# Half-array products of four mixing branches issued in pairs, and products with the meta keys issued last

## The chip, the cores and the metric

The kernel runs on one core of one Trainium2 chip. The metric is the device time of one execution in microseconds (us), the median of several runs. TensorE is written PE, its weight loads PEld; VectorE is DVE, ScalarE is ACT, GpSimd is POOL, SyncE is SP.

## The reference

The model has two blocks; the change touches only the first. Its input is 16 meta tokens followed by 256 tokens, T = 272 rows of 1024, and it runs two layers. In each layer a normed input goes through one wide projection into four mixing branches, whose outputs are gated, summed and projected; a feed-forward part follows. Cut to the branches:

```python
# A: differential attention, 4 heads, two maps m of width 64, values of width 128
s = einsum('bqhmd,bkhmd->bmhqk', q, k) * 64 ** -0.5
p = softmax(s + bias);  a = p[:, 0] - lam * p[:, 1];  o = a @ v
# B: gated linear attention, 4 heads, keys of width 64, values of width 128, chunks of 64, two directions
att = (q_dec @ k_in.T) * causal;  o = att @ v + q_dec @ S_start
# C: latent attention, 4 heads, 128 plain + 64 rotary columns
s = q_nope @ k_nope.T + q_pe @ k_pe.T;  o = softmax(s * 192 ** -0.5) @ v
# D: windowed attention, 8 query heads on 2 key heads of width 64, one sink per head
o = softmax([s_band, s_meta, s_sink]) @ v
```

All four see the 16 meta keys beside the 256 others. The second block (adaptive norms, gated feed-forward parts, a convolution mixer, a pooling mixer with another attention) is unchanged.

## The kernel before, in words

Everything that is multiplied on a large scale (projections, feed-forward parts) is a product split into three parts of the type fp32r (`mm3`: high by high, high by low, low by high); in the profile these are the matmuls whose output is a PSUM buffer `g`. The weights stream in through SP, ACT makes the high part of each (`wh`), DVE the low part (`wl`).

The branches are Python generators (`gen_a` to `gen_d` in `mixing`). A generator emits one step of a branch and yields a number; `tick` resumes it after that many ticks, and between two ticks the main program emits half a tile of a projection, 12 matmuls into `g`. So each engine gets one fixed order in which steps of a branch lie between runs of 12, 24 or 36 matmuls into `g`. Only where the main program needs a branch (`finish`) do its last steps follow each other without such runs between them.

The branches' own products are plain fp32 matmuls into PSUM buffers `a` (`aps`, four buffers; each holds 512 columns of 128 partitions). In the trace each of them is two matmul records, called two passes here. A product whose stationary operand has 64 rows, or whose output has 64 columns, uses half of the PE array; its place follows from the partitions on which operand and output lie.

- Scores (`scores`, and `units`, which runs score, exponential and transpose of successive units one after another): for the query blocks A and B (128 queries each) a unit makes four score tiles 128x272 and DVE adds the bias and takes the maximum (line 566). For block M (the 16 meta queries) one tile holds all four heads, 32 partitions each.
- In `gen_a` a unit is one map m of all four heads: the rows `64*m` to `64*m+63` of `qa` and `ka`. After the second map `close` joins the two, and `transposed` turns the result for the products with the values (`pT` for the 256 tokens, `pm` for the meta keys, `vt` and `vm` the values).
- In `gen_d` and `gen_c` and in the output products of `gen_a` the third product of each head is the one with the meta keys (`pm`, `vm`, 16 rows).
- In `gen_b` heads alternate between rows 0 to 63 and 64 to 127 (`r`), one head after another; `kr` in `gen_c` likewise.

## Time and profile before

| | |
|---|---|
| median of 3 runs | 2278.74 us (2277.09 to 2283.06) |
| profiled execution, its own time | 2284.18 us |
| its span, first to last instruction | 2281.6 us |
| mean granted clock of TensorE | 0.978 of full speed |
| busy: PE, DVE, ACT, POOL | 2192.9, 1612.5, 1217.2, 240.6 us |

Busy times are sums over the span. Matmuls are pipelined: one lasts longer than the step to the next, so time is read from starts of successive rows, not from durations. A row of the timeline merges successive instructions of one form; its first number is the start, its second the time from there to the end of the last.

### The profile page before, as it was taken

The numbers are of one execution on the slowest core, as the hardware profiler recorded it, in microseconds if no ns is written. First come the engines' busy times: TensorE is split into PE (matmuls) and PEld (weight loads), VectorE is DVE, ScalarE is ACT, GpSimd is POOL, SyncE is SP. The second block draws the span as 40 slices with busy tenths as digits, with TensorE's granted clock in tenths as the row PEclk, the third lists the DMA queues.
The fourth block names the chain that finished last, engine by engine and source line by source line (L and its number), as shares of the span: only waits on it lengthen the run. The fifth ranks groups of instructions, "written<-read, shape, count | busy, mean of one in ns | idle before, by whom it ended". The sixth has DMA issues, their size and how long they took to land. (4 is left out here: it accounts for less than half of the span.)

```text
span 2281.6 us, 41972 instructions
## 1 busy us (share of the span) xinstructions
PE 2192.9 (96%) x17048; PEld 2070.0 (91%) x17048; DVE 1612.5 (71%) x2809; ACT 1217.2 (53%) x2221; POOL 240.6 (11%) x285
## 2 busy tenths in 40 slices
PE   7999999999999999999999899986999999999998
PEld 7888888899988798788999799986999999989998
DVE  5655454798885555547989887798877787778553
ACT  4555244577556544445775554465644554466442
POOL 0220111100031001112000100066100000001000
PEclk9999999999999999999999899997999999999999
DMA  7553233454764343324657687733687687744551
GB/s 271 190 183 114 100 102 114 172 206 170 278 242 158 112 148 107 112 97 172 227 184 289 260 302 273 255 111 111 229 283 277 241 303 272 268 174 140 206 177 70
DMA packets 73618, 439.21 MB, mean 192 GB/s; under 512 B 14285, under 2 KB 15629, under 8 KB 25936
## 3 DMA queue, kind: packets, MB, share of 16 engines
q1 hardware_dynamic: 62736, 419.66, 51.3%
q0 software_dynamic: 10400, 16.79, 2.5%
q8 instruction: 133, 2.18, 0.4%
q14 instruction: 61, 0.50, 0.1%
q10 hardware_dynamic: 288, 0.07, 0.0%
HBM read 433.12 MB, written 10.01 MB: 194 GB/s over the span
## 5 line engine op out<-in xcount | busy, mean ns | idle before, releaser
L227 PE MATMUL g<-uh,wh 128*128 128x256 f32 (+2 forms) x3560 | 1034.0, 290 | 18.9 <-ACT uh L322 6.2
L227 PE MATMUL g<-ul,wh 128*128 128x256 f32 (+2 forms) x3560 | 1025.1, 288 | 9.5 <-DVE ul L326 5.9
L227 PE MATMUL g<-uh,wl 128*128 128x256 f32 (+2 forms) x3560 | 1021.8, 287 | 2.7 <-DVE wl L122 2.7
L122 DVE TENSOR_TENSOR wl<-raw,wh 128x1024 fp32r<-128x1024 f32 (+2 forms) x660 | 785.8, 1196 | 274.2 <-ACT wh L114 273.7
L114 ACT ACTIVATE wh<-raw 128x1024 fp32r<-128x1024 f32 (+2 forms) x660 | 670.2, 1020 | 335.5 <-PE g L227 298.9
L227 PEld LDWEIGHTS g<-uh,wh 128*128 128x128 f32 x3560 | 680.1, 191 | 42.2 <-issue 13.5
L227 PEld LDWEIGHTS g<-ul,wh 128*128 128x128 f32 x3560 | 678.7, 191 | 14.0 <-DVE ul L326 6.9
L227 PEld LDWEIGHTS g<-uh,wl 128*128 128x128 f32 x3560 | 680.7, 191 | 3.7 <-DVE wl L122 3.4
L227 PE MATMUL g<-gh,wh 128*128 128x256 f32 (+1 forms) x1056 | 299.2, 283 | 0.0
L227 PE MATMUL g<-gh,wl 128*128 128x256 f32 (+1 forms) x1056 | 299.2, 283 | 0.0
L227 PE MATMUL g<-gl,wh 128*128 128x256 f32 (+1 forms) x1056 | 299.1, 283 | 0.0
L227 PEld LDWEIGHTS g<-gl,wh 128*128 128x128 f32 x1056 | 201.5, 191 | 0.0
L227 PEld LDWEIGHTS g<-gh,wh 128*128 128x128 f32 x1056 | 201.3, 191 | 0.0
L227 PEld LDWEIGHTS g<-gh,wl 128*128 128x128 f32 x1056 | 201.3, 191 | 0.0
L1717 DVE CUSTOM_DVE_ANT_0 adaw<-adaw,condb,vec 128x1024 f32<-128x1024 f32 x144 | 182.4, 1280 | 1.5 <-DMA adaw<-in_ada_t_dram 1.5
L1620 DVE SCALAR_TENSOR_TENSOR y<-edge,vec,y 128x272 f32<-128x272 f32 (+1 forms) x176 | 86.4, 493 | 28.5 <-ACT y L1615 25.4
L227 PE MATMUL g<-oh,wh 128*128 128x272 f32 (+1 forms) x296 | 87.9, 297 | 0.0
L227 PE MATMUL g<-ol,wh 128*128 128x272 f32 (+1 forms) x296 | 84.6, 286 | 0.0
L227 PE MATMUL g<-oh,wl 128*128 128x272 f32 (+1 forms) x296 | 84.5, 285 | 0.0
L1863 ACT ACTIVATE sg<-g 128x256 f32<-128x256 f32 x80 | 30.6, 382 | 99.9 <-PE g L227 99.8
L1224 ACT ACTIVATE gt<-g 128x272 f32<-128x272 f32 (+1 forms) x64 | 25.1, 392 | 107.7 <-PE g L227 107.7
L1252 POOL TENSOR_TENSOR merged<-merged,w 128x272 f32<-128x272 f32 (+1 forms) x48 | 37.9, 798 | 338.5 <-DVE w L1251 338.3
(377 smaller groups left out, 2434.2 us busy)
## 6 DMA issues: line engine op xcount, KB each, us to landing
raw<-in_weights_dram SPq DMA_DIRECT2D x294, 1024.0 KB, 4.9
adaw<-in_ada_t_dram SPq DMA_DIRECT2D x72, 1024.0 KB, 6.6
raw<-in_weights_dram SPq DMA_DIRECT2D x28, 768.0 KB, 4.8
skew<-scr POOLq DMA_DIRECT2D x6, 1086.0 KB, 22.7
h<-skew POOLq DMA_DIRECT2D x8, 544.0 KB, 4.4
h<-skew POOLq DMA_DIRECT2D x8, 512.0 KB, 5.4
condb<-cond SPq DMA_DIRECT2D x5, 512.0 KB, 4.7
hd<-h SPq DMA_DIRECT2D x2, 1088.0 KB, 9.1
```

Of the source, the lines that this page charges most:

```text
L114: self.nc.scalar.activation(h3[:, :, d0 : d0 + n], c.tile[:, :, c0 : c0 + n], AF.Copy)
L122: self.nc.vector.tensor_tensor(out=l3[:, :, d0 : d0 + n], in0=c.tile[:, :, c0 : c0 + n], in1=h3[:, :, d0 : d0 + n].bitcast(F32), op=SUB,)
L227: self.nc.tensor.matmul(out, lhsT, rhs, start=start, stop=stop, skip_group_check=True)
L1224: nc.scalar.activation(t[:, :rn], ps[:, :rn], AF.Tanh, scale=0.5)
L1252: nc.gpsimd.tensor_tensor(out=mg, in0=mg, in1=t, op=ADD)
L1620: nc.vector.scalar_tensor_tensor(out=y, in0=e[:, o : o + on], scalar=cw(i), in1=y, op0=MUL, op1=ADD)
L1717: self.nc.vector.tensor_tensor_reduce(out=t[:, i, :], in0=t[:, i, :], in1=self.condb, scale=1.0, scalar=self.v("ada_b_2", c), op0=MUL, op1 ...
L1863: nc.scalar.activation(t, ps[:, :SEQ], AF.Silu)
```

## The change

In branch A a unit of block A or B becomes two heads with both maps; their four score products go in the order map 0 (rows 0 to 63), map 1 (rows 64 to 127), each into its own buffer (`score.step = 2` tells `scores` to take two buffers at a time). `close` joins the maps in every unit, and `transposed` handles two heads at a time (`pair`), so it runs twice as often on half the data. The bias of such a unit comes in two DMA issues instead of one. In branch D the two heads that share an output buffer alternate. In B two heads alternate on the two row halves, and their output products go by kind. In C the four or two products of a kind go one after another. In A, B, C and D the products with the meta keys come after the others.

```diff
     def scores(...):
-        for i in range(nt):
-            ps = self.aps()
-            score(ps, i)
+        for i0 in range(0, nt, step):
+            pss = [self.aps() for _ in range(step)]
+            score(pss if step > 1 else pss[0], i0)
+            for i, ps in enumerate(pss, i0):
...
     gen_a:
-                    def f(ps, i):
-                        self.mm(ps[:, :T], qa[r, i, q0 : q0 + nq], ka[r, i, :])
+                    def f(pss, i):
+                        h = 2 * m + i // 2
+                        for j, ps in enumerate(pss):
+                            r = slice(64 * j, 64 * j + 64)
+                            self.mm(ps[:, :T], qa[r, h, q0 : q0 + nq], ka[r, h, :])
...
-                for h in range(4):
-                    self.mm(o, pT[:, 0, h, q0 : q0 + nq], vt[:, 0, c], True, False)
-                    self.mm(o, pT[:, 1, h, q0 : q0 + nq], vt[:, 1, c], False, False)
-                    self.mm(o, pm[:, h, q0 : q0 + nq], vm[:, c], False, True)
+                for h, c in enumerate(cs):
+                    self.mm(ps[:nq, c], pT[:, 0, h, q0 : q0 + nq], vt[:, 0, c], h == 0, False)
+                    self.mm(ps[:nq, c], pT[:, 1, h, q0 : q0 + nq], vt[:, 1, c], False, False)
+                for h, c in enumerate(cs):
+                    self.mm(ps[:nq, c], pm[:, h, q0 : q0 + nq], vm[:, c], False, True)
...
     gen_d:
+                    for j in range(3):
+                        for i in range(2):
+                            o = ps[64 * i : 64 * i + 64, :T]
+                            if j < 2:
+                                self.mm(o, vt[:, j, c], pT[:, j, h, :], j == 0, False)
+                            else:
+                                self.mm(o, vm[:, c], pm[:, h, :], False, True)
...
     gen_b:
+                        for r, ps in zip(rows, pss):
+                            self.mm(ps[:, o : o + 128], ki[r, dp, t], qd[r, dp, t])
+                for d_ in range(2):
+                    for r, ps in zip(rows, psm):
+                        self.mm(ps[0:16, o : o + 16], ki[r, dp, 0:16], qd[r, dp, 0:16])
...
     gen_c:
+            def many(os, h0, q0, nq):
+                for h, o in enumerate(os, h0):
+                    self.mm(o, qn[:, h, q0 : q0 + nq], kn[:, h, :], True, False)
+                for h, o in enumerate(os, h0):
+                    self.mm(o, kr[r, 1 + h // 2, q0 : q0 + nq], kr[r, 0, :], False, True)
```

On PE, at the scores of branch C for block A in layer 0, before (a number behind `a_` is a buffer of its own; `kn` has 128 rows, `kr` 64):

```order
L227 MATMUL a_3620<-kn_3360,qn_3359 128x272
L227 MATMUL a_3620<-kr_3323 128x272
L227 MATMUL a_3624<-kn_3360,qn_3359 128x272
L227 MATMUL a_3624<-kr_3323 128x272
L227 MATMUL a_3628<-kn_3360,qn_3359 128x272
L227 MATMUL a_3628<-kr_3323 128x272
L227 MATMUL a_3632<-kn_3360,qn_3359 128x272
L227 MATMUL a_3632<-kr_3323 128x272
```

The same place on PE in the changed kernel:

```order
L227 MATMUL a_3630<-kn_3370,qn_3369 128x272
L227 MATMUL a_3631<-kn_3370,qn_3369 128x272
L227 MATMUL a_3630<-kr_3333 128x272
L227 MATMUL a_3631<-kr_3333 128x272
L227 MATMUL a_3638<-kn_3370,qn_3369 128x272
L227 MATMUL a_3639<-kn_3370,qn_3369 128x272
L227 MATMUL a_3638<-kr_3333 128x272
L227 MATMUL a_3639<-kr_3333 128x272
```

The eight products stand in four groups of a kind instead of eight, and the two `kr` products of a pair, on different row halves, now stand next to each other.

On PE, at the four meta products of branch B's output in layer 0, in the changed kernel (`vm,am` has 16 rows, `st,qdec` 64; before, the two kinds alternated head by head):

```order
L227 MATMUL a_3002<-vm_2556,am_2891 16x128
L227 MATMUL a_3003<-vm_2556,am_2891 16x128
L227 MATMUL a_3002<-vm_2556,am_2891 16x128
L227 MATMUL a_3003<-vm_2556,am_2891 16x128
L227 MATMUL a_3002<-st_2798,qdec_2464 16x128
L227 MATMUL a_3003<-st_2798,qdec_2464 16x128
L227 MATMUL a_3002<-st_2798,qdec_2464 16x128
L227 MATMUL a_3003<-st_2798,qdec_2464 16x128
```

One change of kind is left inside the step, and the `st` products alternate between the two row halves and two buffers.

## Rows read from the trace of the kernel before

**Rows 1.** The page: busy time of each engine, share of the span, instructions.

```profile
PE 2192.9 (96%) x17048; PEld 2070.0 (91%) x17048; DVE 1612.5 (71%) x2809; ACT 1217.2 (53%) x2221; POOL 240.6 (11%) x285
```

**Rows 2.** Stretches: PE, PEld, DVE, ACT, POOL busy, granted clock, DMA share, GB/s.

```profile
76.00:98.00 22.00, 21.84 (x149) 18.90 (x149) 19.19 (x64) 16.41 (x49) 2.41 (x3) 1.00 0.65 233
770.00:792.00 22.00, 21.44 (x144) 18.47 (x143) 16.75 (x53) 15.65 (x47) 0.75 (x1) 1.00 0.38 124
274.00:292.00 18.00, 18.00 (x103) 13.65 (x104) 4.32 (x9) 3.27 (x8) 2.05 (x2) 0.62 0.07 27
900.00:929.00 29.00, 28.41 (x223) 22.35 (x223) 12.46 (x26) 6.23 (x13) 3.49 (x4) 1.00 0.19 64
```

**Rows 3.** Timeline of PE, one unit of scores of branch A, layer 0.

```profile
70.52 2.10 PE L227 MATMUL a<-ka,qa 64*128 64x272 f32 x8
72.55 0.40 PE L227 MATMUL g<-uh,wh 128*128 128x272 f32 x1
```

**Rows 4.** Timeline of PE, scores in the pooling mixer of the second block.

```profile
2020.68 1.14 PE L227 MATMUL a<-k,q 64*128 64x256 f32 x8
2021.75 0.39 PE L227 MATMUL g<-uh,wh 128*128 128x256 f32 x1
```

**Rows 5.** Timeline of PE, scores of the meta queries of branch A.

```profile
62.89 0.66 PE L227 MATMUL a<-ka,qa 64*32 64x272 f32 x8
```

**Rows 6.** Timeline of PE, output products of branch A, blocks M and A.

```profile
101.62 0.61 PE L227 MATMUL a<-v,pT 128*16 128x128 f32 x4
...
102.48 0.61 PE L227 MATMUL a<-v,pT 128*16 128x128 f32 x4
...
106.77 0.71 PE L227 MATMUL a<-v,pT 128*128 128x128 f32 x4
107.41 0.48 PE L227 MATMUL a<-vm,pm 16*128 16x128 f32 x2
107.83 0.71 PE L227 MATMUL a<-v,pT 128*128 128x128 f32 x4
```

**Rows 7.** Timeline of PE, output products of branch D, one pair of heads.

```profile
153.81 1.13 PE L227 MATMUL a<-pT,v 128*64 128x272 f32 x4
154.87 0.67 PE L227 MATMUL a<-pm,vm 16*64 16x272 f32 x2
155.47 1.13 PE L227 MATMUL a<-pT,v 128*64 128x272 f32 x4
```

**Rows 8.** Timeline of PE, attention products of branch B, one head.

```profile
258.61 1.63 PE L227 MATMUL a<-qdec,kin 64*128 64x128 f32 x12
260.17 0.39 PE L227 MATMUL g<-uh,wh 128*128 128x272 f32 x1
```

**Rows 9.** Timeline of PE, output products of branch B, layer 1, blocks M and A.

```profile
914.71 0.37 PE L227 MATMUL a<-vm,am 16*16 16x128 f32 x2 [0.58 <-DVE am L1166]
...
915.33 0.39 PE L227 MATMUL a<-vm,am 16*16 16x128 f32 x2
...
919.76 0.49 PE L227 MATMUL a<-v,acs 128*128 128x128 f32 x2
920.18 0.66 PE L227 MATMUL a<-st,qdec 64*64 64x128 f32 x8
920.77 0.49 PE L227 MATMUL a<-v,acs 128*128 128x128 f32 x2
```

**Rows 10.** Timeline of PE, scores of branch C, blocks M and A.

```profile
330.08 0.65 PE L227 MATMUL a<-kn,qn 128*32 128x272 f32 x2
...
331.23 0.65 PE L227 MATMUL a<-kn,qn 128*32 128x272 f32 x2
...
337.86 0.73 PE L227 MATMUL a<-kn,qn 128*128 128x272 f32 x2
338.51 0.72 PE L227 MATMUL a<-kr 64*128 64x272 f32 x2
339.16 0.73 PE L227 MATMUL a<-kn,qn 128*128 128x272 f32 x2
```

## Prediction

> **What bounds the kernel now.** The first thing to read is the share of busy time: PE is busy for 96% of the span, the next engine, DVE, for 71% [rows 1]. That average hides the mixing layers, so the stretches come next. In 22 us around the scores of branch A in layer 0 PE is busy for 21.8 us, DVE for 19.2 and ACT for 16.4; in layer 1 for 21.4, 16.8 and 15.7 [rows 2]. PE ends last there too, but DVE is close behind it in layer 0. In the output products of branch B in layer 1 DVE has 12.5 of 29 us to do [rows 2].

> A busy PE is not a full PE, so the last view is the timeline of PE, step by step. Three things are to be seen in it.

> First, what a pass costs. The product of branch D with four passes lasts 1.13 us, the one with two 0.67 [rows 7], so a further pass of 272 columns is 0.23 us. With 128 columns the same difference is 0.71 against 0.48 [rows 6], or 0.11 us a pass.

> Second, half-array products that use the same rows or columns do not overlap, and those on different ones do. Eight passes of branch A's scores, all on one row half, take from 70.52 to 72.55, 2.03 us; eight passes of the pooling mixer's scores, whose heads alternate between the row halves and go to separate buffers, take from 2020.68 to 2021.75, 1.07 us [rows 3, 4]. They have 256 columns instead of 272, which over four rounds is some 0.05 us. For columns the meta queries of branch A show it: eight passes of 32 columns each, four places side by side, last 0.66 us in all [rows 5].

> Third, a change of kind (from 128 rows to 16 or 64, or back) stops the stream. One head of branch A's output takes 1.06 us from 106.77 to 107.83 [rows 6]; its six passes at 0.11 are 0.66. The rest, 0.40 us, is the way to the meta kind and back. I use it as the price of one round trip.

> **The change part by part.** The runs of matmuls into `g` between the steps keep their number, so what a step loses on PE is lost from the span, as long as nothing else becomes late. Each saving is for one step, times its number in two layers.

> Scores of A, blocks A and B: eight passes become four rounds of two. Before 2.03 us, after 1.07 + 0.05 = 1.12 [rows 3, 4]: 0.91 us, 8 units, 7.3 us.

> Output of A: for block M a head takes 0.86 us from 101.62 to 102.48; four are 3.43. Grouped: one head's 0.86 and 18 more passes at 0.11, 2.82; saved 0.6, twice, 1.2. For A and B four heads are 4 × 1.06 = 4.24; grouped 1.06 + 18 × 0.11 = 3.04; saved 1.2, 4 times, 4.8 [rows 6]. Together 6.0 us.

> Output of D: one head takes 1.06 us for its `pT` passes and 0.60 for the meta ones [rows 7], and its partner, on the other 64 columns, as much again. Alternating, both run side by side, so one head's 1.66 us goes, less some 0.01 of stagger: 1.65, 8 times, 13.2 us. This is the largest term.

> Attention of B: a head takes 1.56 us, with two trips from the 128-column kind to the 16-column kind [rows 8]. Two heads side by side take the passes of one and one trip less. A trip is bounded by nothing and 0.40; I take 0.2, since the small kind has only 16 columns to load. 1.56 + 0.2 = 1.76 per pair of heads, 4 pairs, 7.0 us. That the runs into `g` are entered half as often there I leave at nothing.

> Output of B: for M a head takes 0.62 us from 914.71 to 915.33, four 2.5; grouped 0.62 + 6 × 0.11 for the 16-row kind + 2 × 0.11 for the paired 64-row kind = 1.5; saved 1.0, twice. For A and B a head takes 1.01 us from 919.76, 0.42 of it up to the 64-row kind at 920.18 and 0.59 in it [rows 9]. There the column halves already overlap; after, four quarters do, so eight rounds serve four heads: 0.42 + 6 × 0.11 + 0.59 + 4 × 0.11 = 2.1 against 4.0; saved 1.9, 4 times. Together 9.6 us.

> Scores of C: for M a head takes 1.15 us from 330.08 to 331.23; four heads on four column places at once need little more than one: saved 3.4, twice. For A and B a head takes 0.65 us in each kind [rows 10]; a pair takes 0.65 + 2 × 0.23 for the full products, then 0.65 for both half ones: 1.76 instead of 2.60, saved 0.84, 8 pairs, 6.7. Together 13.5 us.

> Output of C: two heads share one round trip, 0.40, 4 pairs: 1.6 us.

> The sum is 7.3 + 6.0 + 13.2 + 7.0 + 9.6 + 13.5 + 1.6 = 58.2 us.

> What is added: per unit of A one more DMA issue on POOL, which is busy 11% of the span; per block two more, smaller evictions on ACT and one tiny multiply on DVE. They are hidden where DVE and ACT have room. In layer 0 DVE hardly has: three units of scores lie in 76 to 98 us, and 22 us less 3 × 0.91 is 19.3, against DVE's 19.2 [rows 2]. The transposes of A also come after every unit, so PE meets DVE's scaling four times a layer instead of twice. Nothing lost is the one end; all 7.3 us of A's scores and some in B (the wait for `am`, 0.58 us now [rows 9], has the work of two heads ahead of it in DVE's queue) the other, some 12 us. I take 3 us, near the lower end, because layer 1 has 16.8 us of DVE work for 19.3 us and the output steps right after give the queue time to empty.

> That leaves 55 us. The profiled execution's own 2284.2 less 55 is 2229; it lies 5.4 us above the median of the runs shown, so the forecast for the median is 2224 us.

> [...] In the changed scores of C the four `kr` products of block M use both row halves and write one buffer; in every other pair the row halves write separate buffers, as the rows of the pooling mixer do [rows 4]. No row here shows two row halves writing one buffer at a time. [...] If these rounds went one after the other instead, two more rounds of 0.23 us in each layer, 0.9 us, would be missing from the sum.

> **The rivals.** *Waits take more.* If A's units become bound by DVE and ACT in both layers and B waits longer for `am`, 12 us go: 46 us saved, 2233. For it speaks 19.2 of 22 us in layer 0; against it the 16.8 and 15.7 of layer 1 [rows 2].

> *The slow stretch goes away.* From 274 to 292 us, in B's output of layer 0, the granted clock averages 0.62; the same steps in layer 1, 900 to 929, ran at 1.00 [rows 2]. 18 × 0.38 is 6.8 us lost. Denser steps may keep the clock up there: 2217. Or the fall may move to another place, which changes nothing.

> *The pairs do not overlap.* Then only the grouping pays: A's and C's output keep 6.0 + 1.6; A's scores nothing; D gives back six passes a step, 2.2 left; B's attention gives back eight passes and the small ones, 2.8 left; B's output 5.2; C's scores 4.3. That is 22 us, 2257. Rows 3 and 4 differ in just this and speak against it.

> *Slower.* If the packed steps made the clock fall, work would take twice as long while it is down. 55 us more need some 110 us at half clock, eight times the 13.7 us that the mean of 0.62 over 18 us stands for [rows 2]; above that the kernel is slower than before, say 2290. For it speaks that the fall at 274 us came among half-array products. Against it: the same products ran at 1.00 in layer 1, and the change makes the share of full-array matmuls in these stretches larger. [...]

> **How the numbers follow.** The forecast 0.59 (its own range 2217 to 2231: waits from nothing to 10 us), more waits 0.15, the slow stretch gone 0.13, no overlap 0.05, slower 0.03; the last 0.05 is a partial overlap, between 2240 and 2257. The range from 2209 to 2239 holds the first three with 2 to 8 us of scatter and leaves out about 0.13. About 0.3%, 7 us, is what a measurement of this kernel can tell from no change: faster by more 0.96, within it 0.01, slower 0.03.

> **What would show it.** In the timeline after: A's scores x8 in some 1.12 us to the next `g`; D's output as one x8 of `pT` and one x4 of `pm` in 1.7 us; C's meta scores in 1.2 instead of 4.6; B's attention steps half as many. Wrong would be: x8 of `ka,qa` still 2 us (no overlap); rows of the transposes at the changed line with waits of over 0.5 us in most units of A (waits); a granted clock under 0.9 in stretches where it was 1.00.

## The result: 2219.6 us, 2.6% faster

The changed kernel takes 2219.61 us (median of 4 runs, 2218.51 to 2221.20), the kernel before 2278.6 beside it (4 runs, 2277.09 to 2283.06): a ratio of 0.9742, 95% interval 0.9726 to 0.9758. The forecast was 2224 within 2209 to 2239, so the kernel gained 59 us where 55 were forecast. The profiled execution took 2218.51 us, its span is 2216.7 us at a mean granted clock of 0.982.

The page of the changed kernel, its line of busy times; PE still has 96% [rows 1], of a shorter span:

```profile
PE 2127.1 (96%) x17048; PEld 2039.7 (92%) x17048; DVE 1611.7 (73%) x2813; ACT 1215.1 (55%) x2225; POOL 245.9 (11%) x293
```

The timeline of PE in the changed kernel (start, time to the end of the last, engine, line, operation and tiles, rows*columns, shape, count, idle time before and its releaser). In order: two units of A's scores and transposes behind them, A's output for blocks M and A, D's output, B's attention, C's scores for blocks M and A, C's output for two heads, and B's output in layer 1 for blocks M and A. The `g` row behind a step shows when it is over:

```profile
73.17 1.19 PE L227 MATMUL a<-ka,qa 64*128 64x272 f32 x8
74.29 0.39 PE L227 MATMUL g<-uh,wh 128*128 128x272 f32 x1
...
78.44 1.18 PE L227 MATMUL a<-ka,qa 64*128 64x272 f32 x6
80.09 0.72 PE L227 MATMUL a<-ka,qa 64*128 64x272 f32 x2 [0.46 <-ACT pm L653]
80.74 0.39 PE L227 MATMUL g<-uh,wh 128*128 128x272 f32 x1
...
83.18 0.66 PE L662 MATMUL a<-ident,s 128*128 128x128 f32 x4 [0.66 <-DVE mx L568]
...
99.08 1.92 PE L227 MATMUL a<-v,pT 128*16 128x128 f32 x16
...
101.90 0.40 PE L227 MATMUL g<-uh,wh 128*128 128x272 f32 x1
...
103.52 1.95 PE L227 MATMUL a<-v,pT 128*128 128x128 f32 x16
...
106.48 0.39 PE L227 MATMUL g<-uh,wh 128*128 128x272 f32 x1
...
149.21 1.14 PE L227 MATMUL a<-pT,v 128*64 128x272 f32 x8
150.28 0.67 PE L227 MATMUL a<-pm,vm 16*64 16x272 f32 x4
150.88 0.39 PE L227 MATMUL g<-uh,wh 128*128 128x272 f32 x1
...
247.39 1.36 PE L227 MATMUL a<-qdec,kin 64*128 64x128 f32 x24
248.68 0.40 PE L227 MATMUL g<-uh,wh 128*128 128x272 f32 x1
...
302.42 0.67 PE L227 MATMUL a<-kn,qn 128*32 128x272 f32 x8
303.02 0.66 PE L227 MATMUL a<-kr 64*32 64x272 f32 x8
303.61 0.39 PE L227 MATMUL g<-oh,wh 128*128 128x272 f32 x1
...
306.74 1.08 PE L227 MATMUL a<-kn,qn 128*128 128x272 f32 x4
307.75 0.73 PE L227 MATMUL a<-kr 64*128 64x272 f32 x4
308.41 1.18 PE L227 MATMUL a<-kn,qn 128*128 128x272 f32 x4
...
310.18 0.40 PE L227 MATMUL g<-uh,wh 128*128 128x272 f32 x1
...
328.89 2.00 PE L227 MATMUL a<-pT,v 128*128 128x272 f32 x8
...
331.93 0.39 PE L227 MATMUL g<-oh,wh 128*128 128x272 f32 x1
...
863.97 1.03 PE L227 MATMUL a<-vm,am 16*16 16x128 f32 x8
...
865.47 0.39 PE L227 MATMUL g<-uh,wh 128*128 128x272 f32 x1
...
867.09 1.05 PE L227 MATMUL a<-v,acs 128*128 128x128 f32 x8
868.07 1.10 PE L227 MATMUL a<-st,qdec 64*64 64x128 f32 x32
869.11 0.39 PE L227 MATMUL g<-uh,wh 128*128 128x272 f32 x1
```

The steps of before, where the rows ahead of the prediction show only one or two heads of them: A's output for block A, C's scores for block A, C's output for one head, and B's output in layer 1, the end of block M (it begins at 914.71 [rows 9]) and block A, each from its first row to the `g` row behind it:

```profile
105.82 0.61 PE L227 MATMUL a<-v,pT 128*128 128x128 f32 x4
...
109.94 0.40 PE L227 MATMUL g<-uh,wh 128*128 128x272 f32 x1
...
336.65 0.62 PE L227 MATMUL a<-kn,qn 128*128 128x272 f32 x2
...
341.78 0.40 PE L227 MATMUL g<-uh,wh 128*128 128x272 f32 x1
...
362.18 1.08 PE L227 MATMUL a<-pT,v 128*128 128x272 f32 x4
...
363.84 0.39 PE L227 MATMUL g<-oh,wh 128*128 128x272 f32 x1
...
917.23 0.40 PE L227 MATMUL g<-uh,wh 128*128 128x272 f32 x1
...
918.86 0.38 PE L227 MATMUL a<-v,acs 128*128 128x128 f32 x2
...
922.79 0.39 PE L227 MATMUL g<-uh,wh 128*128 128x272 f32 x1
```

Read from the start of a step to the first `g` row behind it, at full clock and without the waits (B's output for block B lies at 924.39 to 928.27 before and at 870.72 to 872.73 after):

| step | before, us | after, us | saved | forecast |
|---|---|---|---|---|
| A scores, a unit [rows 3] | 2.03 | 1.12 | 0.91 × 8 = 7.3 | 7.3 |
| A output, M; A or B | 3.43; 4.12 | 2.82; 2.96 | 0.61 × 2 + 1.15 × 4 = 5.8 | 6.0 |
| D output, two heads [rows 7] | 2 × 1.66 | 1.67 | 1.65 × 8 = 13.2 | 13.2 |
| B attention, two heads [rows 8] | 2 × 1.56 | 1.29 | 1.83 × 4 = 7.3 | 7.0 |
| B output, M; A; B | 2.53; 3.93; 3.88 | 1.50; 2.02; 2.01 | 1.03 × 2 + 1.91 × 2 + 1.87 × 2 = 9.6 | 9.6 |
| C scores, M; four heads of A or B | 4.59; 5.13 | 1.19; 3.44 | 3.40 × 2 + 1.69 × 4 = 13.6 | 13.5 |
| C output, two heads | 2 × 1.66 | 3.04 | 0.28 × 4 = 1.1 | 1.6 |

Together that is 57.9 us where the prediction had 58.2. Against it stand the new waits in branch A: the view of waits for PE from 60 to 200 us, first before (total, times, longest):

```profile
PE a L643 <- DVE mx L566: 1.2, 1, 1.2
PE a L657 <- DVE mx L566: 0.2, 1, 0.2
```

and the same view of the changed kernel:

```profile
PE a L648 <- DVE mx L568: 1.6, 2, 1.2
PE a L662 <- DVE mx L568: 0.7, 1, 0.7
PE a L662 <- DVE s L913: 0.6, 2, 0.4
PE a L227 <- ACT pm L653: 0.5, 1, 0.5
```

The 1.2 us at the first line is a wait in branch D that stands in both. The rest grew from 0.2 to 2.2 us (0.4 + 0.7 + 0.6 + 0.5). A wait also costs more than its idle time: the unit at 78.44 us lasts 2.30 us instead of 1.12, for 0.46 us of idle time.

### The profile page after: what moved, and what is told of

It reads as the page before. It is cut to its first block, busy times and chain, and to the rows that moved or that the text cites. A ratio compares the mean times of both kernels' runs of the same rounds, so it can differ in the third digit from the quotient of the medians.

```text
span 2216.7 us, 42006 instructions
## 1 busy us (share of the span) xinstructions
PE 2127.1 (96%) x17048; PEld 2039.7 (92%) x17048; DVE 1611.7 (73%) x2813; ACT 1215.1 (55%) x2225; POOL 245.9 (11%) x293
```

## The experiments

All are the changed kernel with one edit, unless said, and are timed beside the kernel before, whose median was 2277 to 2278 us each time (single runs 2275.5 to 2284.0). "More" and "come back" are differences of medians to the changed kernel's 2219.6 us, unless said. The mean granted clock of a run matters at this size: 0.001 of the span is 2.2 us, and the runs of one kernel differ by 0.001 to 0.005; two executions of the kernel before, at 0.978 and 0.981, have spans 6.9 us apart.

### The changed kernel once more

No edit; it is the measure for three of the runs below: the row halves of B apart, and the longer pace a second time and in both layers.

> The changed kernel unchanged, as the measure for the other three on the same chip: 2219.6 us, 2218 to 2222.

2219.3 us (2216.47 to 2221.45), ratio 0.9739 (0.9721 to 0.9757). The result stands; the two medians of the changed kernel differ by 0.3 us, single runs by 5.

### The largest term undone: D's output as before

```diff
-                    for j in range(3):
-                        for i in range(2):
-                            h = 2 * pr + i
-                            ...
+                    for i in range(2):
+                        h = 2 * pr + i
+                        o = ps[64 * i : 64 * i + 64, :T]
+                        self.mm(o, vt[:, 0, c], pT[:, 0, h, :], True, False)
+                        self.mm(o, vt[:, 1, c], pT[:, 1, h, :], False, False)
+                        self.mm(o, vm[:, c], pm[:, h, :], False, True)
```

> The changed kernel with branch D's output as it was before (head by head, the meta product of each right behind it). My theory: the whole 1.65 us a step comes back and nothing else moves: eight steps, 13.2 us, 2233 us. Rival: part of what the traces show as D's share was given back elsewhere (a later step waited), then less than 11 us comes back.

2230.93 us (2229.62 to 2232.39), ratio 0.9792 (0.9779 to 0.9806): 11.3 us over the changed kernel by the medians, between the two expectations. In its trace each of the eight steps takes 3.32 us again, 13.2 us more in all, and its waits in A's scores are no longer than in the changed kernel (0.21 us for 0.46). So the steps come back whole; the 1.9 us by which the medians fall short are within what the runs scatter and the clock differs (0.983 to 0.984 here, 0.981 to 0.983 in the changed kernel).

### Is it the turn or the kind? D head by head, meta products last

```diff
-                    for j in range(3):
-                        for i in range(2):
-                            ...
+                    for i in range(2):
+                        h = 2 * pr + i
+                        o = ps[64 * i : 64 * i + 64, :T]
+                        for j in range(2):
+                            self.mm(o, vt[:, j, c], pT[:, j, h, :], j == 0, False)
+                    for i in range(2):
+                        h = 2 * pr + i
+                        self.mm(ps[64 * i : 64 * i + 64, :T], vm[:, c], pm[:, h, :], False, True)
```

> The changed kernel, except that in branch D's output the four pT products of a step are issued head by head (both of the first head, then both of the second) instead of in turn; the meta products still come last. My theory: PE takes products in their order, and a product on other columns starts only once the one ahead of it has started, so overlap needs neighbours on different places. Then only the last pass of the first head runs beside the first pass of the second: a step takes seven passes of 0.23 us one behind the other instead of four, 0.69 us more, eight steps, 5.5 us: 2225 us. Rival one: PE looks past waiting products, and only the change of kind matters: no change, 2220 us, and eight passes in the time of four. Rival two: nothing of the two heads overlaps: 0.93 us a step, 7.4 us, 2227.

2220.74 us (2216.42 to 2222.20), ratio 0.9744 (0.9729 to 0.9759): no change, and my theory falls. The timeline of PE in this kernel:

```profile
147.89 1.15 PE L227 MATMUL a<-pT,v 128*64 128x272 f32 x8
148.97 0.68 PE L227 MATMUL a<-pm,vm 16*64 16x272 f32 x4
149.57 0.39 PE L227 MATMUL g<-uh,wh 128*128 128x272 f32 x1
```

Eight passes take 1.08 us to the next row, as they do in turn (1.07, from 149.21 to 150.28). The second head starts 14 ns behind the first, although three passes of the first head stand ahead of it in the program; in turn it is 7 ns. So PE passes over products that wait for their place; the records carry no head, but two passes on the same columns start 0.23 us apart, so passes that start together belong to two heads. What kept the two heads apart before was the meta product between them, which is of another kind. That it was not merely the number of passes between shows in block M of C's scores before: there the next head's `kn` product, on other columns, also has three passes waiting ahead of it, two of them `kr`, and it starts only when these have gone, 1.15 us behind the first [rows 10].

### How far does PE look? B's output, row half after row half

```diff
-                    for hp in range(2):
-                        for d_ in range(2):
-                            for h in (2 * hp, 2 * hp + 1):
+                    for h in (0, 2, 1, 3):
+                        for d_ in range(2):
+                            r, hp = rows[h % 2], h // 2
+                            for cc in range(2):
                                 ...
```

> The changed kernel, except that in the output of branch B (blocks A and B) the 64-row products are issued head by head in the order 0, 2, 1, 3: first all eight (six in block B) of the upper row half, then all of the lower, instead of in turn. It asks how far PE looks past products that wait for their place; one was passed in the D order head by head. If it looks past any number, nothing changes: 2219.6 us. If it passes only one or two, the row halves follow each other almost wholly: eight and six more rounds of 0.11 us in each layer, 3.1 us, 2222.7, and the starts in the trace come in twos (the two column halves) instead of fours.

2222.97 us (2219.72 to 2224.21), ratio 0.9754 (0.9736 to 0.9771), 3.7 us over the changed kernel timed with it (2219.3). The timeline of PE at block A in layer 0:

```profile
260.11 1.59 PE L227 MATMUL a<-st,qdec 64*64 64x128 f32 x32
261.63 0.40 PE L227 MATMUL g<-uh,wh 128*128 128x272 f32 x1
```

The step lasts 1.52 us, in the changed kernel 1.04 (868.07 to 869.11). Half the loss of a wholly serial order (eight rounds of 0.11, 0.9 us) came: neither theory. The single records of the trace say why. These are starts of passes in us; the first 16 of the program are of the upper row half, rows 0 to 63:

```
260.106 .113 | .266 .273 | .375 .382 | .484 .491 | .593 .600 | .606 .613 | .703 .709 | .766 .773 | .812 .818 | ...
```

Five rounds of two go, 0.11 us apart but for the first. Right behind the fifth, 6 ns later, another two start, with a record of 0.32 us like the first two of the step, where all between have 0.27. I read them as the first of the lower half; from there two sequences run side by side. At that moment six of the sixteen passes were still waiting, so PE passed over six here.

That is no fixed reach. In block B's step of the same trace (from 264.228 us) the upper half has twelve passes, and the two that begin the lower half start 0.493 and 0.500 us in, with three left; from 0.435 us on four had been waiting, and the lower half did not start. In both steps it starts some 0.5 us in, behind the fifth pass on one quarter of the array; what sets this stays open. The two kinds of step lose 0.49 and 0.48 us, four of them 1.9; the medians differ by more, with runs that overlap.

### Pairing apart from grouping: C's pairs on the same row half

```diff
-                        many([ps[:, :T] for ps in pss], i, q0, nq)
+                        many([ps[:, :T] for ps in pss], (0, 2, 1, 3)[i : i + 2], q0, nq)
```

The buffers of block M and the reads in C's output follow the same order of heads.

> The changed kernel, except that blocks A and B of branch C's scores take the heads in the order 0, 2, 1, 3, so that the two kr products of a pair use the same row half instead of different ones; kinds are grouped as in the changed kernel, and everything else is the same work. It parts pairing from grouping. My theory: the second kr product waits for the first, two more passes of 0.23 us a pair, eight pairs, 3.7 us: 2223 us. Rival: the overlap of these single pairs brings nothing beyond the grouping, since the change of kind back to g hides the second product: no change, 2220.

2222.78 us (2221.17 to 2225.50), ratio 0.9752 (0.9735 to 0.9769): 3.2 us more, where 3.7 were expected; the difference is near the scatter, the trace shows it directly. The timeline of PE, one pair:

```profile
306.68 1.08 PE L227 MATMUL a<-kn,qn 128*128 128x272 f32 x4
307.69 1.18 PE L227 MATMUL a<-kr 64*128 64x272 f32 x4
308.80 1.18 PE L227 MATMUL a<-kn,qn 128*128 128x272 f32 x4
```

The four `kr` passes take 1.11 us on one row half and 0.66 (307.75 to 308.41) on two, 0.45 a pair, 3.6 in all. The pairing pays for itself even where only two products stand together.

### C's scores as before

```diff
-            def many(os, h0, q0, nq):
-                ...
+            def one(o, h, q0, nq):
+                r = slice(64 * (h % 2), 64 * (h % 2) + 64)
+                self.mm(o, qn[:, h, q0 : q0 + nq], kn[:, h, :], True, False)
+                self.mm(o, kr[r, 1 + h // 2, q0 : q0 + nq], kr[r, 0, :], False, True)
```

> The changed kernel with the scores of branch C as before (one head at a time, both kinds). My theory: 3.4 us in each of the two M steps and 0.84 us in each of eight pairs come back, 13.5 us, 2233 us. Rival: DVE's reductions, which come two by two behind a pair now, hide some of it, so that the blocks A and B give back less: 6.8 us for M alone, 2226.

2231.75 us (2230.96 to 2232.43), ratio 0.9796 (0.9782 to 0.9809): 12.1 us come back. That is far from the 6.8 of block M alone, so the rival is out. In its trace C's scores take 29.7 us instead of 16.1, 13.6 more, so the steps of blocks A and B come back whole too.

### B's products as before

```diff
-            for hp in range(2):
-                pss = [self.aps(), self.aps()]
-                ...
+            for h in range(4):
+                r = slice(64 * (h % 2), 64 * (h % 2) + 64)
+                ps = self.aps()
+                ...
```

The output products are put back head by head in the same way.

> The changed kernel with branch B's attention and output products as before. My theory: its own passes come back. By the steps of the two traces at full clock that is 4.1 us a layer for the attention (four steps of 1.78 against two of 1.51), 1.5 for the meta block's output and 3.8 for the other two blocks: 19 us in two layers, 2238.5 us. Rival: the slow stretch of the clock at 274 to 292 us in the profile of the kernel before belongs to these half-array products and comes back with them, 6.8 us more: 2245, and a granted clock of some 0.6 in that stretch of this run's profile.

2242.14 us (2237.18 to 2244.20), ratio 0.9833 (0.9814 to 0.9851): 22.5 us come back, between 19 and 25.8. The rival is out: B's output lies at 260.9 to 274.5 us in this kernel's profile, and the clock was 1.00 all around it.

```profile
250.00:300.00 50.00, 49.42 (x383) 42.42 (x381) 23.99 (x51) 17.96 (x41) 5.74 (x5) 1.00 0.24 84
```

The wait for `am` is back in this kernel's view of waits (two times 0.6), but the 1.5 us expected for the meta block held it already: 1.03 in the step and 0.51 of wait. So the 3.5 us above 19 are not settled; the runs of this kernel scatter by 7 us, at a lower clock (0.978 to 0.982).

### Is the slow stretch always there? The kernel before, a second profile

No edit.

> The kernel before, unchanged, for a second profile. It asks whether the stretch at half clock from 274 to 288 us is there in every execution. My theory: it is not, since the granted clock falls at places that move between executions; then the changed kernel's gain from it being gone in its profile (about 6.8 us of the profiled difference) is not in the difference of the medians. Rival: it stands at the same place, with a granted clock of some 0.62 over 274 to 292 us.

2276.49 us, span 2274.7, mean clock 0.981 (0.978 in the first profile). The window of this second profile:

```profile
274.00:292.00 18.00, 18.00 (x154) 15.66 (x154) 8.07 (x16) 6.86 (x15) 3.06 (x3) 1.00 0.09 30
```

The same program ran that stretch at 1.00 instead of 0.62 [rows 2]. The spans differ by 6.9 us, and the mean clocks say the same: 2281.6 × 0.022 less 2274.7 × 0.019 is 7.0 us. PE had done the same steps before it in both. So this fall belongs to the one execution, and does not come with the kernel's steps as such.

### What the new waits cost: A's units as before

```diff
-                    def f(pss, i):
-                        h = 2 * m + i // 2
-                        ...
+                    def f(ps, i):
+                        self.mm(ps[:, :T], qa[r, i, q0 : q0 + nq], ka[r, i, :])
```

`close`, the transposes and the loads of the bias go back with it.

> The changed kernel with the units of branch A as before (a unit is one map of four heads, scaling and transposes once for two units, loads of the bias as before); its output products stay grouped. It measures the waits that the new units brought. My theory: 0.91 us in each of eight units is lost again, 7.3 us, and 3.4 us of new waits go: 4 us, 2223.5. Rival: the waits cost as much as the pairing brought, no change, 2219.6, or the waits that the trace shows were there before anyhow: 7.3 us, 2227.

2223.86 us (2223.67 to 2228.56), ratio 0.9769 (0.9755 to 0.9784): 4.2 us more, as expected. Its view of waits from 60 to 200 us has the two lines of before and no other:

```profile
PE a L648 <- DVE mx L568: 1.2, 1, 1.2
PE a L662 <- DVE mx L568: 0.2, 1, 0.2
```

So the pairing brought 7.3 us by its steps and the units that go with it took about 3.1 back, by difference; with runs up to 2228.56 that is good to a us or two.

### Taking the waits away: a longer pace in layer 0

```diff
-    def units(self, todo, transposed, close=None):
+    def units(self, todo, transposed, close=None, pace=1):
...
-            yield 1
+            yield pace
             if ended is not None and ended[0] is not None:
...
+                2 if l == 0 else 1,
```

The last line is the argument in `gen_a`.

> The changed kernel, except that in layer 0 branch A's units leave twice as many matmuls into g between a unit's scores and the transposes of the unit before it (24 instead of 12), so that the branch takes longer and DVE and ACT get more time. My theory: the waits of 3.4 us that PE has there (0.66 us for DVE ahead of the transposes at 83 us, 0.46 for ACT's copy at 80 us, and others) go, nothing else moves, and the kernel beats the changed one: 2216.5 us. Rival: the matmuls that are used up there are missing as cover behind branch A, where the output products and the heads' norms wait instead: no change or slower, 2220 to 2224.

2214.44 us (2213.16 to 2217.34), ratio 0.9716 (0.9699 to 0.9733): 5.2 us below the changed kernel. Its windows show where; 66 to 98 us in the changed kernel, then here (PE, PEld, DVE, ACT, POOL busy, clock, DMA share, GB/s):

```profile
66.00:98.00 32.00, 29.81 (x219) 25.27 (x219) 28.18 (x86) 23.33 (x65) 5.60 (x8) 1.00 0.68 234
```

```profile
66.00:98.00 32.00, 32.00 (x251) 28.59 (x250) 28.00 (x82) 23.02 (x61) 5.35 (x8) 1.00 0.72 251
```

DVE does as much as in the changed kernel, and PE is never idle (2.2 us there): it has more `g` work while DVE and ACT finish a unit. The view of waits has none of branch A's units left from 60 to 200 us, and branch D's 1.2 us became another of 0.8:

```profile
PE a L227 <- DVE qm L1019: 0.8, 1, 0.8
```

### The same, beside the changed kernel

> The version with the longer pace in layer 0 alone, once more, beside the changed kernel on the same chip, since its gain is near what the runs scatter. My theory: 2.5 us of waits are gone by the trace, so 2 to 5 us below the changed kernel. Rival: the gain was scatter, within 1 us of it.

2215.52 us (2213.87 to 2217.01), ratio 0.9723 (0.9706 to 0.9740), against 2219.3 for the changed kernel: 3.8 us. The gain is there, in medians 5.2 and 3.8 us, though single runs overlap. The waits in the trace account for about 3: the unit of scores that lasted 2.30 us takes 1.12 again, 1.2, and the other waits of branch A, 1.7. The rest is not settled; the mean clock is up to 0.001 higher in these runs.

### The same in both layers

```diff
-                2 if l == 0 else 1,
+                2,
```

> The changed kernel with twice as many matmuls into g between a unit's scores and the transposes before it in branch A of both layers. In layer 1 the trace of the changed kernel has one wait of 0.31 us there. My theory: layer 1 has little to gain, so this stands where layer 0 alone stood, 2214 to 2216 us. Rival: the matmuls used up in layer 1 are missing as cover later: slower than that by over 2 us.

2214.62 us (2212.54 to 2215.20), ratio 0.9719 (0.9703 to 0.9736): as in layer 0 alone, within the scatter. Nothing is lost as cover, and there was little to gain.

## Why the prediction was right

**The pairs overlap.** Right, and to the hundredth where a row of the same work stood before: A's unit takes the 1.12 us that the pooling mixer's row gave [rows 3, 4]. The rival that they do not overlap is out, by C's pairs on one row half too.

**D.** 13.2 us as forecast, the largest term, and undoing it brings it back. The reason was only half right. I put the gain down to alternating the heads; the run head by head shows that the turn is not needed, only that no product of another kind stands between (a step takes 3.32 us with the meta product between the heads, 1.68 head by head with it last, 1.67 in turn). So the rival's arithmetic, in which grouping alone saves 2.2 us in D, would not have held either: grouping alone makes the pairs here.

**The other steps.** The sum of the steps was right, 57.9 us for 58.2, and the large terms are right one by one: A's and C's scores, D's and B's output. Three smaller ones were off, and nearly cancel. B's attention saved 7.3 for 7.0: 1.83 us a pair of heads less 1.56 leaves 0.27 for the trip that I put at 0.2; a weight load of the small kind does last less, 91 ns for 64*16 against 186 for 64*128 in the trace of the kernel before. A's output saved 5.8 for 6.0: I took four heads of before as 4 × 1.06, but the first head of a step takes 0.95 (105.82 to 106.77), so the step was 4.12 and not 4.24. C's output saved 1.1 for 1.6: I took the price of a trip from A's rows, 0.40, and there it was 0.28. No run put A's or C's output back, so these two terms are read from the traces alone.

In B's attention the entries into `g`, half as many, come on top; I had left them at nothing. In the timeline a `g` pass follows the last by 0.13 us, but a step's first pass follows the last `g` pass by 0.22, and behind a step the second `g` pass comes 0.23 after the first: some 0.2 us an entry, four fewer, 0.8 us. C's output has four fewer too; its first pass follows the last `g` pass by 0.12 like another `g` pass, so they save 0.1 each, 0.4 us.

**The waits.** 3 us forecast, about 3.1 by putting A's units back, a difference of medians. That they agree to 0.1 is luck: I chose 3 between nothing and 12. Place and cause were as argued: DVE in layer 0, with 28.18 us of work in 32. One wait was not foreseen: at 80.09 us the scores wait not for DVE but for ACT, whose copy of block M's transposes holds one of the four buffers. And one that I had feared went the other way: before, the products of `vm,am` waited 0.58 us for `am` [rows 9], twice in all; in the changed kernel the row at 863.97 has no wait beside it, and with B's products as before the wait is back, 1.2 us in two times in the view of waits. From the last `g` pass to the step it was 0.87 us and is 0.36, so the two gave 1.0 us.

**Two row halves into one buffer.** The four `kr` products of C's block M use both row halves and write one buffer. The first passes of all four start within 20 ns (303.019 to 303.039), and the next row begins 0.59 us after the first of the eight (303.02 to 303.61), less than four passes of a pair into separate buffers take (0.66). Rounds one after the other, which the prediction put at 0.9 us in all, would have added 0.23 us each; no such time is there in this case, in which the four write different partitions of the buffer. Two row halves on the same partitions were not tried.

**The slow stretch.** It is gone in the profile after, as that rival had it, and still adds nothing to the result: the kernel before had it in one profiled execution and not in the other, at nearly the median time. The rival of the slower side is out: the mean clock is 0.982 after and 0.978 and 0.981 before. Its factor of two at half clock was too high as well. In the kernel before, the work in B's output from the last head of block M up to block B took 13.70 us at a granted clock of 0.50 in layer 0 (274.24 to 287.94) and 7.79 at 1.00 in layer 1 (916.60 to 924.39): 1.76 times as long, 5.9 us lost and not 6.8.

**The size.** The kernel came out 4.4 us under the forecast, within its range. The steps gave 57.9, B's entries 0.8, C's 0.4, the waits for `am` 1.0; less 3.1 for A's waits that is 57.0 us, where the medians differ by 59.0. The 2 us between are not settled: the mean clock of the runs is 0.981 before and 0.982 after, which can hold them, and no run shows whether that belongs to the change. The 5.4 us that I took off between the profiled 2284.18 and the median were right to take off: the second profile, at 2276.49, lacks the slow stretch.

## What to carry to other kernels

Where half-array matmuls stand among others, look first for what stands between two of them that could share the array: a product of another kind costs time (some 0.3 to 0.4 us a round trip here) and cuts the overlap (D's step takes 3.32 us with one between the heads, 1.68 with it last), while a few passes that merely wait for their place are passed over. So sort by kind first, and keep products on different rows or columns close to each other: with three passes between nothing was lost, with twelve or sixteen 0.48 us a step. Strict alternation is not needed for that. When PE's steps get shorter, give DVE and ACT the time back by putting other matmuls between a step and its consumer: here the version with the longer pace (medians 2214.4 to 2215.5 us) came out some 4 to 5 us below the changed kernel, of which the waits in the trace account for about 3.
